# Fetching expert tokens by index: slots by rank, rows from a DRAM copy of x, and a selection by comparison

## The chip, the core and the metric

The kernel runs on one core of a Trainium2 chip. The metric is the time of one execution on the device, in microseconds; the time before is the median of three runs. A profile of one execution gives, for each engine, its instructions with start, length and what they waited for. TensorE is PE in the rows (its weight loads PEld), VectorE DVE, ScalarE ACT, GpSimd POOL, and SP is the engine whose queue issues most DMAs.

## The reference

Two layers over 512 tokens of 1024 columns, in float32. Each layer adds to x an attention branch, a mixture of experts and a gated embedding. The change is in the mixture of experts, where each of 16 experts takes the 64 tokens with the largest affinity to it:

```python
def expert_choice_moe(h, w_router, w1, w3, w2):
    cap = EC_CAPACITY * S // N_EXPERTS                  # 64
    aff = jax.nn.softmax(einsum('bsd,de->bse', h, w_router), axis=-1)
    vals, idx = lax.top_k(aff.transpose(0, 2, 1), cap)  # of each expert
    xg = h[bidx, idx]
    out = (silu(xg @ w1[e]) * (xg @ w3[e])) @ w2[e]
    return zeros_like(h).at[bidx, idx].add(out * vals[..., None])
```

Here h is x after an RMS norm; the expert weights are 1024 x 1024 each, three for each expert.

## The kernel before

x stays in SBUF as four blocks of 128 tokens. The whole program is ordered by a scheduler that runs its own simulation of the engines: within each engine the order is fixed at build time, and a step goes where that simulation finds it ready. `tc.issue_after` only holds a step back behind another one.

**Weights.** `w_tile` issues each 1 MB tile of expert weights as one DMA on SP's queue (L540). The tiles live in a ring of 15 slots (the pool `s8`, shared with a few other tiles), with six more in two small pools for some of the early tiles. A DMA waits until the products that read the slot's last tile are done, so the ring is freed by TensorE, and SP's queue is in order. The first tiles are loaded during the output product of the attention (`GATED`).

**Slots and gathers.** A token's slot at an expert is a number from 1 to 64. For expert 0 it is its rank: the affinities of expert 0 are spread over all partitions by matmuls (L572, the tiles `rowp`), VectorE (L579) and ScalarE (a Sign pass, L580) count greater and equal ones, and `pos0` results. `warm` puts idle matmuls on TensorE over such waits. For the other experts the affinities are transposed (L618), and eight rounds of MAX8 (L628) and MATCH_REPLACE8 (L630) on VectorE mark the 64 largest; a scan over the marks in the order of the sequence gives slots, which four small transposes (L641) bring to `pos`. `gather_one` gathers one expert's tokens: a selection matrix from `iota` and `pos` (L591), times x (L602), copied and transposed (L611, L612). Experts 0 to 3 use it (`ONE`). The other twelve come in two gathers of six (`gather`): x is normalised and split into two parts for each of eight blocks of columns (L682 on ScalarE, L683 on VectorE) and eight matmuls for each block select all six experts' tokens (L686). Gather A is made after expert 3, gather B before expert 7 (`GATHER_B`), and the scheduler lays their blocks between the experts' products.

**Experts.** `hidden(e)` forms tokens times w1 and w3 (L703, 64 matmul records an expert), the SwiGLU (L707 to L709) and its transposes (L712, the tile gT). `down(e)` forms the product with w2 for experts 0 to 3 (L723), whose outputs `scatter` adds to x after expert 7. Experts 4 to 15 keep their activations; their w2 comes afterwards in four quarters of 256 columns (L862, L866), each followed by the scatter (L881) and, beside it, by the gated embedding's products. `where(pr)` gives the scatter its selection for a pair of experts: comparisons with `pos` (L656), four transposes (L659), and the affinities by four small products (L664).

**Queues.** SP issues the weights, ScalarE's queue the biases and the constant `before`. GpSimd issues no DMA; in the experts' stage it has no work before the last sums of the layer.

## Time and profile before

| | us |
|---|---|
| median of 3 runs | 1981.12 |
| range of the runs | 1980.59 to 1981.26 |
| span of the profiled execution | 1978.8 |
| TensorE busy in it | 1901.6 |
| VectorE busy | 778.2 |
| ScalarE busy | 600.8 |
| GpSimd busy | 99.7 |

The profiled span stands 2.3 us under the median of the runs. The two layers have the same course, the second some 977 us after the first; most rows are of the first. In it the experts' first products run from 458 to 798 us, and the four quarters of w2 from there to some 970. TensorE's busy time counts matmuls by modelled ends, and a matmul that is pipelined with the one before it overlaps it, so lengths are read off starts or off busy time by stretch.

### The profile page before, as it was taken

What the parts mean: (1) busy time and instruction counts of PE and PEld (TensorE: products, weight loads), DVE (VectorE), ACT (ScalarE), POOL (GpSimd) and SP (SyncE); (2) the same over time, 40 slices, a digit from 0 to 9 for tenths busy, and PEclk for the clock granted to TensorE, in tenths of its full rate; (3) what the DMA queues carried; (4) which work ended last, traced back from release to release, by engine and by line L of the source; (5) the groups of instructions that cost most, each with busy time, mean ns of one, the idle gap of its engine ahead of it and who ended that gap; (6) DMA issues with size and microseconds to landing.
All of it is one profiled execution on the core that took longest, in us unless ns stands there. A gap on an engine that the chain in (4) does not pass through costs nothing.

```text
span 1978.8 us, 26755 instructions
## 1 busy us (share of the span) xinstructions
PE 1901.6 (96%) x10700; PEld 1239.0 (63%) x10700; DVE 778.2 (39%) x1638; ACT 600.8 (30%) x1257; POOL 99.7 (5%) x156
## 2 busy tenths in 40 slices
PE   7999999999999999999899999999999999999995
PEld 7777777894353333666697677789933533336664
DVE  4655343435141410323657554444342413103336
ACT  3655343331131111231346454433201411112222
POOL 0012110000000000000200121100000000000002
PEclk9999999999999999999999999999999999899998
DMA  5220322479989999989332112234899899999891
GB/s 162 65 75 22 102 80 85 160 287 383 404 339 370 420 419 420 388 318 342 108 102 78 54 46 84 74 98 181 345 358 394 320 411 420 420 413 388 310 322 73
DMA packets 246043, 486.69 MB, mean 246 GB/s; under 512 B 9248, under 2 KB 164384, under 8 KB 245920
## 3 DMA queue, kind: packets, MB, share of 16 engines
q1 hardware_dynamic: 243040, 478.71, 64.7%
q10 hardware_dynamic: 2880, 6.29, 1.0%
q8 instruction: 84, 1.38, 0.3%
q14 instruction: 39, 0.32, 0.0%
HBM read 482.87 MB, written 2.10 MB: 245 GB/s over the span
## 4 chain that ended last, share of the span: by engine, by line
PE 91%; DVE 6%; ACT 1%; issue 1%; DMA 0%; SPq 0%; DVEq 0%; ACTq 0%
PE t L703 22%; PE po L866 9%; PE tokp L152 6%; PE xo L152 5%; PE op L152 5%; PE pg L152 4%; PE po L723 3%; PE sca L881 3%; PE gat L686 2%; PE o L386 2%; PE tp L379 2%; PE gat L602 1%; PE pw L152 1%; PE s L366 1%; PE o L442 1%; PE s L152 1%
## 5 line engine op out<-in xcount | busy, mean ns | idle before, releaser
L703 PE MATMUL t<-w,xg 128*64 128x512 f32 x2048 | 457.5, 598 | 1.6 <-DVE xg L612 1.6
L703 PEld LDWEIGHTS t<-w,xg 128*64 128x64 f32 x2048 | 142.9, 137 | 279.0 <-issue 271.5
L167 DVE TENSOR_TENSOR wl<-raw,wh 128x1024 fp32r<-128x1024 f32 (+2 forms) x116 | 134.6, 1161 | 185.6 <-ACT wh L97 185.0
L866 PE MATMUL po<-s,s 128*64 128x256 f32 x1536 | 188.7, 383 | 0.0
L97 ACT ACTIVATE wh<-raw 128x1024 fp32r<-128x1024 f32 (+2 forms) x116 | 116.7, 1006 | 111.1 <-PE tokp L152 19.7
L866 PEld LDWEIGHTS po<-s,s 128*64 128x64 f32 x1536 | 108.9, 137 | 59.7 <-issue 6.5
L152 PE MATMUL tokp<-wh,s 128*128 128x256 f32 (+1 forms) x640 | 120.4, 287 | 0.0
L708 DVE SCALAR_TENSOR_TENSOR u<-u,t 128x512 f32<-128x512 f32 x32 | 21.9, 686 | 218.0 <-ACT u L707 218.0
L152 PEld LDWEIGHTS tokp<-wh,s 128*128 128x128 f32 x640 | 102.5, 196 | 2.2 <-issue 1.5
L152 PE MATMUL pg<-s,hp 128*128 128x512 f32 x384 | 101.1, 406 | 1.1 <-ACT hp L97 1.1
L152 PE MATMUL xo<-wh,s 128*128 128x256 f32 x512 | 94.9, 285 | 0.0
L152 PE MATMUL tokp<-wl,s 128*128 128x256 f32 (+1 forms) x320 | 91.4, 287 | 0.5 <-DVE wl L167 0.5
L922 POOL TENSOR_TENSOR x<-x,s 128x512 f32<-128x512 f32 x16 | 23.8, 1511 | 1343.1 <-DVE s L920 1338.7
L152 PEld LDWEIGHTS pg<-s,hp 128*128 128x128 f32 x384 | 68.6, 188 | 24.8 <-issue 7.7
L709 DVE TENSOR_TENSOR u<-u,t 128x512 f32<-128x512 f32 x32 | 21.9, 684 | 155.6 <-PE t L703 155.6
L152 PE MATMUL op<-s,wh 128*128 128x512 f32 x256 | 82.2, 397 | 0.0
L152 PEld LDWEIGHTS xo<-wh,s 128*128 128x128 f32 x512 | 80.3, 192 | 0.1
L707 ACT ACTIVATE u<-t 128x512 f32<-128x512 f32 x32 | 19.1, 598 | 195.0 <-PE t L703 195.0
L872 ACT ACTIVATE oh<-po,val 128x256 fp32r<-128x256 f32 x48 | 22.8, 475 | 174.6 <-PE po L866 174.2
L152 PE MATMUL xo<-wl,s 128*128 128x256 f32 x256 | 72.1, 285 | 0.0
L873 DVE SCALAR_TENSOR_TENSOR oh<-po,val,oh 128x256 fp32r<-128x256 f32 x48 | 23.2, 483 | 124.2 <-ACT oh L872 124.2
L152 PEld LDWEIGHTS tokp<-wl,s 128*128 128x128 f32 x320 | 62.5, 195 | 2.1 <-DVE wl L167 1.1
(470 smaller groups left out, 3173.7 us busy)
## 6 DMA issues: line engine op xcount, KB each, us to landing
w<-in_moe_w_dram SPq DMA_DIRECT2D x288, 1024.0 KB, 11.0
s<-in_moe_w_dram SPq DMA_DIRECT2D x96, 1024.0 KB, 10.6
raw<-in_w_in_dram SPq DMA_DIRECT2D x64, 512.0 KB, 3.7
raw<-in_w_out_dram SPq DMA_DIRECT2D x16, 512.0 KB, 3.3
s<-in_ple_gate_w_dram SPq DMA_DIRECT2D x8, 1024.0 KB, 10.4
bias<-in_bias_dram ACTq DMA_DIRECT2D x16, 320.0 KB, 3.1
raw<-in_w_mla_o_dram SPq DMA_DIRECT2D x8, 512.0 KB, 3.3
raw<-in_w_na_o_dram SPq DMA_DIRECT2D x8, 512.0 KB, 3.3
```

The source lines that it names most:

```text
L97: sc.activation(o, i, AF.Copy, scale=scale)
L152: pe.matmul(ps, s_, m_, start=(i == 0), stop=(i == n - 1))
L167: ve.tensor_sub(wl, raw, wh.bitcast(F32))
L379: pe.transpose(tp[:, j, :], pr_[:, j * P:(j + 1) * P], ident)
L386: pe.matmul(o[hh_ * 64:(hh_ + 1) * 64, :], vm[:, j, h * 64:(h + 1) * 64], pts[hh_][:, j, :], start=(j == 0), stop=(j == 3))
L686: pe.matmul(ps, (xh if i % 2 == 0 else xl)[:, i // 2, :], s[:, i // 2].rearrange("p a b -> p (a b)"), start=(i == 0), stop=(i == 7))
L703: products.append(pe.matmul(ps[hf * 64:(hf + 1) * 64, :], xg(k), w[:, k % 2, hf * S:(hf + 1) * S], start=(k == 0), stop=(k == 7)))
L723: pe.matmul(po[hf * 64:(hf + 1) * 64, :], gT[:, k % 4, k // 4, :], w[:, k % 2, hf * S:(hf + 1) * S], start=(k == 0), stop=(k == 7))
L866: pe.matmul(po[ee * CAP:(ee + 1) * CAP, :], gTs[2 * n + ee][:, k % 4, k // 4, :], ws[ee][:, k, :], start=(k == 0), stop=(k == 7))
L873: ve.scalar_tensor_tensor(o[:, 1, :], po, val, o[:, 0, :].bitcast(F32), ALU.mult, ALU.subtract)
L881: pe.matmul(ps[:, j, :], sT[:, (c + j) * P:(c + j + 1) * P], o, start=(i == 0), stop=(i == len(parts) - 1))
L922: (gp if 2 * c + hf in (LAST_POOL if last else ON_POOL) else ve).tensor_tensor(xv, xv, t, ALU.add)
```

## The change

Slots of the first pair (`RANKED = 2`) go by rank: `ranks(e)` is the old code of expert 0 as a function, called for expert 1 too, after the first gather. Only these two experts are gathered by `gather_one`. `before` and `iota` keep their use there.

For all experts the eight rounds now keep the values and, by `max_index`, the places of the 64 largest; the loop's last replacement, the scan and the four small transposes go. Places are turned from the order of the sequence to the order of the kernel's tokens by shifts, and two small products per half bring values and places to `vals`, `places` and `index`, one column for each pair of experts, 128 slots on the partitions.

x is copied to DRAM (`xd`, rows of 1024 columns and one more that holds the token's norm factor `rx`), by eight DMAs on ScalarE's queue. `fetch(pr)` is an indirect DMA on GpSimd's queue that reads the 128 rows of a pair of experts. `turn(pr)` multiplies each row by its factor, transposes it in eight blocks and multiplies by the gains. The fetches of pairs 1 and 2 are issued before the first expert, and each following one when a pair has been turned; a turn is held back behind the products of the last expert of the pair before. The two big gathers go.

`where` compares a new constant, the tokens' numbers, with `places`, which gives the selection in the orientation that the scatter needs; its transposes, its ScalarE copy and the value products go. The rest of the diff takes out comments, renames `GATHER_B` to `SCATTER_AT`, and sets GpSimd's DMA scratch to 2048 bytes.

```diff
+RANKED = 2
...
+    dp = ctx.enter_context(tc.tile_pool(name="dram", bufs=2, space=bass.MemoryType.DRAM))
...
+            gains, lgains, iota, wr, number = (load(n) for n in ("gains", "lgains", "iota", "w_router", "number"))
...
+        xd = dp.tile([S, D + 1], F32, tag="xd", name="xd")
+        for c in range(4):
+            sc.dma_start(xd[c * P:(c + 1) * P, 0:D], x[:, c, :])
+        for c in range(4):
+            sc.dma_start(xd[c * P:(c + 1) * P, D:D + 1], rx[:, c:c + 1])
...
+        def ranks(e):
...
         xg = gather_one(0)
+        for e in range(1, RANKED):
+            ranks(e)
...
-        for _ in range(CAP // 8):
-            m8 = kp.tile([NE, 8], F32, tag="m8", bufs=2, name="m8")
-            ve.max(m8, cur)
-            nxt = row()
-            ve.match_replace(nxt, m8, cur, -1.0)
-            cur = nxt
-        sel = row()
-        ve.tensor_scalar(sel, cur, 0.0, None, ALU.is_lt)
-        cs = row()
-        ve.tensor_tensor_scan(cs, sel, sel, 0.0, ALU.add, ALU.max)
-        ps1 = row()
-        ve.tensor_tensor(ps1.rearrange("e (c r) -> e r c", r=GH), cs.rearrange("e (r c) -> e r c", r=GH),
-                         sel.rearrange("e (r c) -> e r c", r=GH), ALU.mult)
-        pT = psT.tile([P, 4, NE], F32, tag="T", name="pT")
-        for c in range(4):
-            pe.transpose(pT[:, c, :], ps1[:, c * P:(c + 1) * P], ident[:NE, :NE])
-        ve.tensor_copy(pos, pT)
-        ve.tensor_copy(pos[:, :, 0], pos0)
-        if dbg and l == 0:
-            dma(dbg["pos"], pos.rearrange("p c e -> p (c e)"))
-            dma(dbg["aff"], aff.rearrange("p c e -> p (c e)"))
+        best = kp.tile([NE, 2, CAP], F32, name="best")
+        place = kp.tile([NE, CAP], U32, name="place")
+        for i in range(CAP // 8):
+            s_ = slice(8 * i, 8 * i + 8)
+            ve.max(best[:, 0, s_], cur)
+            ve.max_index(place[:, s_], best[:, 0, s_], cur)
+            if i < CAP // 8 - 1:
+                nxt = row()
+                ve.match_replace(nxt, best[:, 0, s_], cur, -1.0)
+                cur = nxt
+        part = kp.tile([NE, CAP], U32, name="part")
+        ve.tensor_scalar(part, place, GW - 1, GH.bit_length() - 1, ALU.bitwise_and, ALU.logical_shift_left)
+        ve.scalar_tensor_tensor(place, place, GW.bit_length() - 1, part, ALU.logical_shift_right, ALU.bitwise_or)
+        ve.tensor_copy(best[:, 1, :], place)
+        pv = psT.tile([P, 2, NE // 2], F32, tag="T", name="pv")
+        for i in range(2):
+            for j in range(2):
+                pe.matmul(pv[j * CAP:(j + 1) * CAP, i, :], best[:, i, :], ident[:NE, j:NE:2], start=(i == 0), stop=(i == 1), skip_group_check=True)
+        vals = ep.tile([P, NE // 2], F32, bufs=1, name="vals")
+        places = ep.tile([P, NE // 2], F32, bufs=1, name="places")
+        index = ep.tile([P, NE // 2], U32, bufs=1, name="index")
+        ve.tensor_copy(index, pv[:, 1, :])
+        ve.tensor_copy(places, pv[:, 1, :])
+        ve.tensor_scalar(vals, pv[:, 0, :], 0.5, None, ALU.mult)
...
         def where(pr):
-            sv = qp.tile([P, 4, 2, CAP], F32, tag="oh", bufs=OHB, name="sv")
-            for c in range(4):
-                ve.tensor_tensor(sv[:, c], bc(pos[:, c, 2 * pr:2 * pr + 2], CAP), iota.unsqueeze(1).to_broadcast([P, 2, CAP]), ALU.is_equal)
-            ps = psT.tile([P, S], F32, tag="T", name="tp")
-            for c in range(4):
-                pe.transpose(ps[:, c * P:(c + 1) * P], sv[:, c].rearrange("p a b -> p (a b)"), ident)
             svT = qp.tile([P, S], F32R, tag="svT", bufs=(NE - BLOCKED) // 2, name="svT")
-            acopy(svT, ps)
-            ps = psT.tile([P, 2], F32, tag="T", name="val")
-            for c in range(4):
-                pe.matmul(ps, sv[:, c].rearrange("p a b -> p (a b)"), aff[:, c, 2 * pr:2 * pr + 2], start=(c == 0), stop=(c == 3))
-            val = qp.tile([P, 1], F32, tag="val", bufs=(NE - BLOCKED) // 2, name="val")
-            for ee in range(2):
-                r = slice(ee * CAP, (ee + 1) * CAP)
-                ve.tensor_scalar(val[r, :], ps[r, ee:ee + 1], 0.5, None, ALU.mult)
-            return svT, val
-        def gather(pool, e0, n):
-            xg = pool.tile([P, 8, n * CAP], F32, tag="xg", bufs=1, name="xg")
-            s = ga.tile([P, 4, n, CAP], F32R, tag="sel", bufs=1, name="sel")
-            for c in range(4):
-                ve.tensor_tensor(s[:, c], bc(pos[:, c, e0:e0 + n], CAP), iota.unsqueeze(1).to_broadcast([P, n, CAP]), ALU.is_equal)
-            for k in range(8):
-                xh = ga.tile([P, 4, P], F32R, tag="xh", name="xh")
-                xl = ga.tile([P, 4, P], F32R, tag="xl", name="xl")
-                for c in range(4):
-                    xv = x[:, c, k * P:(k + 1) * P]
-                    sc.activation(xh[:, c, :], xv, AF.Identity, scale=rx[:, c:c + 1])
-                    ve.scalar_tensor_tensor(xl[:, c, :], xv, rx[:, c:c + 1], xh[:, c, :].bitcast(F32), ALU.mult, ALU.subtract)
-                ps = psS.tile([P, n * CAP], F32, tag="S", name="gat")
-                for i in range(8):
-                    pe.matmul(ps, (xh if i % 2 == 0 else xl)[:, i // 2, :], s[:, i // 2].rearrange("p a b -> p (a b)"),
-                              start=(i == 0), stop=(i == 7))
-                if k % 2:
-                    sc.activation(xg[:, k, :], ps, AF.Identity, scale=g_moe[:, k:k + 1])
-                else:
-                    ve.tensor_scalar(xg[:, k, :], ps, g_moe[:, k:k + 1], None, ALU.mult)
+            ve.tensor_scalar(svT, number, places[:, pr:pr + 1], None, ALU.is_equal)
+            return svT, vals[:, pr:pr + 1]
...
+        def fetch(pr):
+            rows_ = gp_.tile([P, D + 1], F32, tag="rows", bufs=2, name="rows")
+            gp.indirect_dma_start(out=rows_, out_offset=None, in_=xd, in_offset=bass.IndirectOffsetOnAxis(ap=index[:, pr:pr + 1], axis=0))
+            return rows_
+        def turn(rows_):
+            xg = gp_.tile([P, 8, 2 * CAP], F32, tag="xg", bufs=2, name="xg")
+            ve.tensor_scalar(rows_[:, 0:D], rows_[:, 0:D], rows_[:, D:D + 1], None, ALU.mult)
+            for q in range(2):
+                ps = psT.tile([P, 4, P], F32, tag="T", name="tp")
+                for j in range(4):
+                    k = 4 * q + j
+                    pe.transpose(ps[:, j, :], rows_[:, k * P:(k + 1) * P], ident)
+                ve.tensor_tensor(xg[:, 4 * q:4 * q + 4, :], ps, bc(g_moe[:, 4 * q:4 * q + 4], P), ALU.mult)
...
+        fetched = {pr: fetch(pr) for pr in (RANKED // 2, RANKED // 2 + 1)}
+        turned = {}
+        def tokens(e):
+            if e < RANKED:
+                return xg[e]
+            return lambda k: turned[e // 2][:, k, e % 2 * CAP:(e % 2 + 1) * CAP]
+        def next_tokens(e):
+            pr = e // 2 + 1
+            if e % 2 and pr in fetched:
+                with tc.issue_after(products[-1].ins):
+                    turned[pr] = turn(fetched.pop(pr))
+                if pr + 2 < NE // 2:
+                    fetched[pr + 2] = fetch(pr + 2)
...
-            if e < ONE - 1:
+            if e + 1 < RANKED:
                 with tc.issue_after(products[-1].ins):
-                    xg = gather_one(e + 1)
-            else:
+                    xg.append(gather_one(e + 1))
+            next_tokens(e)
+            if e == ONE - 1:
...
-        xgA = gather(ga, ONE, NA_)
...
-            gT = hidden(e, lambda k: xg[:, k, i * CAP:(i + 1) * CAP], kept if e >= BLOCKED else None)
+            gT = hidden(e, tokens(e), kept if e >= BLOCKED else None)
+            next_tokens(e)
...
-    nc = bacc.Bacc("TRN2", target_bir_lowering=False, num_devices=1)
+    nc = bacc.Bacc("TRN2", target_bir_lowering=False, num_devices=1, dynamic_dma_scratch_size=2048)
```

## Rows read from the trace of the kernel before

**Rows 1.** The page: the span; TensorE's busy time, its share and its matmuls; the share of the DMA engines in tenths, over 40 equal slices of the span.

```profile
span 1978.8 us, 26755 instructions
...
PE 1901.6 (96%) x10700; PEld 1239.0 (63%) x10700; DVE 778.2 (39%) x1638; ACT 600.8 (30%) x1257; POOL 99.7 (5%) x156
...
DMA  5220322479989999989332112234899899999891
```

**Rows 2.** Busy time by stretch. Columns: the stretch in us and its length; busy us and instructions of TensorE (PE), its weight loads (PEld), VectorE (DVE), ScalarE (ACT) and GpSimd (POOL); the granted TensorE clock; the busy share of the DMA engines; GB/s. The first six rows are of layer one, the last three of layer two.

```profile
443.00:463.00 20.00, 19.25 (x143) 13.60 (x144) 12.75 (x43) 4.43 (x12) 0.00 (x0) 1.00 0.84 332
463.00:546.00 83.00, 79.30 (x376) 27.79 (x374) 27.47 (x64) 8.84 (x20) 0.00 (x0) 1.00 0.99 401
546.00:612.00 66.00, 66.00 (x324) 35.89 (x322) 26.58 (x74) 24.57 (x70) 0.00 (x0) 1.00 0.87 333
612.00:796.00 184.00, 174.23 (x784) 65.42 (x780) 33.77 (x63) 23.43 (x37) 0.00 (x0) 0.98 1.03 419
796.00:842.00 46.00, 44.88 (x348) 30.57 (x348) 14.40 (x39) 10.76 (x23) 0.00 (x0) 1.00 1.08 387
842.00:884.00 42.00, 42.00 (x298) 28.99 (x296) 10.85 (x18) 12.82 (x28) 0.00 (x0) 1.00 0.86 305
...
1440.00:1523.00 83.00, 79.29 (x370) 27.59 (x368) 26.18 (x61) 8.84 (x20) 0.00 (x0) 0.98 1.00 401
1523.00:1590.00 67.00, 67.00 (x330) 36.27 (x328) 28.19 (x80) 24.58 (x70) 0.00 (x0) 1.00 0.87 326
1590.00:1774.00 184.00, 174.53 (x782) 65.99 (x780) 33.77 (x63) 23.44 (x37) 0.00 (x0) 0.97 1.03 419
```

**Rows 3.** The waits of SP's DMA queue from 460 to 620 us: which line waited for whom, us in total, times, the longest. L540 issues the expert weights, t is written by the first products (L703), po by the second (L723).

```profile
SPq L540 <- PE t L703: 110.0, 46, 15.9
SPq L540 <- PE po L723: 32.9, 11, 7.6
```

**Rows 4.** The waits of TensorE's weight loads from 740 to 800 us, the row on DMA, with the same columns.

```profile
PEld t L703 <- DMA w<-in_moe_w_dram: 1.0, 2, 0.8
```

**Rows 5.** TensorE's instructions in order of time, in layer one, merged where alike: start, length (us), engine, line, operation, tiles, shape, count, and in brackets the idle time before and what ended it. First the start of the experts' stage, then its end and the end of the first quarter of w2.

```profile
458.31 13.95 PE L703 MATMUL t<-w,xg 128*64 128x512 f32 x64
474.99 0.39 PE L641 MATMUL pT<-ident,row 16*128 16x16 f32 x4 [2.73 <-DVE row L637]
475.31 0.66 PE L712 MATMUL gT<-ident,u 128*128 128x128 f32 x4
...
488.05 13.95 PE L703 MATMUL t<-w,xg 128*64 128x512 f32 x64 [0.78 <-DVE xg L612]
...
506.75 7.09 PE L723 MATMUL po<-w,gT 128*64 128x512 f32 x32
...
768.50 13.95 PE L703 MATMUL t<-w,xg 128*64 128x512 f32 x64
...
783.89 14.06 PE L703 MATMUL t<-w,xg 128*64 128x512 f32 x64
...
833.64 3.67 PE L866 MATMUL po<-s,s 128*64 128x256 f32 x30
...
838.25 1.70 PE L881 MATMUL sca<-oh,svT 128*128 128x256 f32 x12
```

**Rows 6.** Busy time of TensorE by single lines, each asked for alone over a stretch (columns: stretch, length, PE busy, PEld busy, clock, DMA share, GB/s). In this order: the matmuls of the big gathers (L686); of the one-expert gathers after the first (L602); their transposes (L611); the selection's transposes (L659) in the scatter of the first pairs and in the first quarter; the selection's value products (L664) in the same two places; the rows of the first rank (L572).

```profile
458.00:800.00 342.00, 24.41 (x128) 21.91 (x128) 0.99 0.98 393
...
458.00:800.00 342.00, 11.87 (x48) 3.58 (x48) 0.99 0.98 393
...
458.00:800.00 342.00, 2.41 (x12) 1.23 (x12) 0.99 0.98 393
...
640.00:675.00 35.00, 1.73 (x8) 1.28 (x8) 1.00 1.03 421
...
798.00:842.00 44.00, 3.86 (x24) 2.65 (x24) 1.00 1.08 387
...
640.00:675.00 35.00, 2.18 (x16) 2.13 (x16) 1.00 1.03 421
...
798.00:842.00 44.00, 5.89 (x48) 5.82 (x48) 1.00 1.08 387
...
443.00:463.00 20.00, 2.02 (x16) 1.86 (x16) 1.00 0.84 332
```

**Rows 7.** Groups of VectorE instructions by line, tile and shape: count, busy us, mean ns of one, and the idle time before them.

```profile
L167 DVE TENSOR_TENSOR wl<-raw,wh 128x1024 fp32r<-128x1024 f32 x96 | 117.6, 1225 | 166.5 <-ACT wh L97 166.1
...
L628 DVE MAX8 m<-row 16x8 f32<-16x512 f32 x16 | 10.9, 681 | 0.6
...
L630 DVE MATCH_REPLACE8 row<-m,row 16x512 f32<-16x512 f32 x16 | 10.6, 662 | 0.0
```

**Rows 8.** ScalarE's instructions in order of time: two DMA issues on its queue, and the first Sign pass of the first rank, with the idle time before it.

```profile
321.59 0.98 ACTq L547 DMA_DIRECT2D before<-in_before_dram  x2
...
449.00 0.66 ACT L580 ACTIVATE junk<-rowp,na 128x512 f32<-128x512 f32 x1 [2.93 <-PE rowp L572]
```

**Rows 9.** The DMAs issued on L540 over the whole span: us from issue to landing, least, median and most.

```profile
DMA to landing us min/median/max: 4.7/11.0/18.8
```

**Rows 10.** Busy time by stretch around the embedding's product in layer one, columns as in rows 2.

```profile
718.00:722.00 4.00, 1.12 (x5) 0.60 (x5) 2.75 (x4) 2.49 (x3) 0.00 (x0) 1.00 1.02 420
...
724.00:730.00 6.00, 5.75 (x14) 2.59 (x14) 0.00 (x0) 0.80 (x2) 0.00 (x0) 0.50 1.03 422
```

More of the change, by code (lines that the diff above doesn't have):

```diff
@@ L562, in trunk @@
         ve.tensor_tensor(aff, lgs, bc(sm, NE), ALU.mult)
-        warm(WARM[1], m_lg)
-        rowp = []
-        for _ in range(2):
-            rowp.append(psT.tile([P, S], F32, tag="T", name="rowp"))
-            for c in range(4):
-                m = pe.matmul(rowp[-1][:, c * P:(c + 1) * P], aff[:, c, 0:1].to_broadcast([P, P]), ident, start=(c == 0), stop=(c == 3), skip_group_check=True)
-        warm(WARM[0], m)
-        na = small.tile([P, 4], F32, tag="nm4", name="na")
-        ve.tensor_scalar(na, aff[:, :, 0], -2.0 ** 60, None, ALU.mult)
@@ L576, in trunk @@
-        junk, junk2 = (psS.tile([P, S], F32, tag="S", name="junk") for _ in range(2))
-        rank = small.tile([P, 2, 4], F32, tag="ss16", name="rank")
-        for c in range(4):
-            ve.scalar_tensor_tensor(junk, rowp[0], aff[:, c, 0:1], before[c // 2][:, c % 2, :], ALU.is_equal, ALU.mult, accum_out=rank[:, 0, c:c + 1])
-            sc.activation(junk2, rowp[1], AF.Sign, scale=2.0 ** 60, bias=na[:, c:c + 1], accum_out=rank[:, 1, c:c + 1])
-        pos0 = ep.tile([P, 4], F32, bufs=1, name="pos0")
@@ L761, in trunk @@
         gTs, pw = [], []
+        gt = ExitStack()
+        gp_ = gt.enter_context(tc.tile_pool(name=f"ga{l}", bufs=2, side="right", reuse_waits="tile"))
+        fetched = {pr: fetch(pr) for pr in (RANKED // 2, RANKED // 2 + 1)}
[11 more added lines that the diff above has]
+                    fetched[pr + 2] = fetch(pr + 2)
+        xg = [xg]
         for e in range(ONE):
[L764 removed]
+            gT = hidden(e, tokens(e))
             if e % 4 == 0 and e < BLOCKED:
                 outputs()
[L767 removed]
+            if e + 1 < RANKED:
                 with tc.issue_after(products[-1].ins):
[L769 to L770 removed]
+                    xg.append(gather_one(e + 1))
+            next_tokens(e)
+            if e == ONE - 1:
                 ft.close()
@@ L969, in _constants @@
         "iota": np.tile(np.arange(1, CAP + 1, dtype=f), (P, 1)),
+        "number": np.tile(np.arange(S, dtype=f), (P, 1)),
     }
```

50 lines of the change are left out of this document (27 added, 23 removed).

## The prediction

> **What bounds the kernel now.** I read the page first: TensorE (PE) is busy for 96% of the span, and the DMA line stands near full in the ten slices of each layer that hold the mixture of experts [rows 1]. Two resources near their limit mean that the average decides nothing, so I cut the expert stage into stretches. The reader is to see in each row whether PE or the DMA engines have room. From 463 to 546 us the engines move 401 GB/s, from 546 to 612 only 333, from 612 to 796 again 419 with a share of 1.03 [rows 2]. I take 420 GB/s as what they can do with these 4 KB rows. The dip lies where the big gather A stands on PE. Why the queue stops there is in its own waits: between 460 and 620 us SP waits 110.0 us for the expert products and 32.9 us for the second products to free a buffer [rows 3]: the ring is full because PE spends its time on gathers. At the other end the reverse holds. The last expert's products take 14.06 us where others take 13.95, and the weight loads wait 1.0 us for DMA there [rows 4, 5]: the last weights come just in time. So in the hidden stage (first products to the last expert's, 458.31 to 797.95, 339.6 us) both end together, and work taken from PE is worth only what DMA can follow. After that come four quarters of w2. The first runs at 387 GB/s with a DMA share of 1.08, the limit for its 1 KB rows. The second has PE busy 42.00 of 42 us and a share of 0.86: PE sets its end [rows 2]. What is won up to the end of the first quarter is kept.
>
> **The change, part by part, for one layer.**
>
> *PE.* Gone in the hidden stage: gathers A and B, 128 matmuls, 24.4 us; two of three one-expert gathers of that stretch, 2/3 of 11.87 = 7.9, with their transposes, 2/3 of 2.41 = 1.6; the selection's transposes and value products inside the scatter of the first pairs, 1.73 + 2.18 = 3.9 [rows 6]; the 2.73 us wait for the selection after the first expert and the 0.78 us wait before the second [rows 5], as expert 1 now has its slots by rank, ready before the first products end. Sum 41.3. The product that turns values and places replaces the four small transposes behind that wait, at their 0.39 us. Added: seven pairs with two groups of four transposes, each 0.66 like the four of gT [rows 5], 9.2; the second rank's rows, 2.0 as for the first [rows 6]. Net 30.1. In the first quarter six more selections go: 3.86 + 5.89 = 9.75 [rows 6]. New on the path of each pair is the scaling of the fetched rows on VectorE: the nearest row is a 128x1024 operation, 1.23 us [rows 7]. If none of it is covered, seven cost 8.6. PE's stage is then 309.5 to 318 us.
>
> *DMA, weights.* The same weights move. Without the dips the stretch 463 to 796 needs 333 us less 83 x 19/420 = 3.8, less 66 x 87/420 = 13.7, less 0.4: 17.9 less, 315.1 us. In layer two the same rows give 3.8 + 15.0 + 0.4 = 19.2. Lower bound for this gain: nothing, if the ring blocks as before; I take the whole, because a tile waits for products some fourteen tiles of the ring back, those of experts 2 and 3 where the dip begins, and PE reaches these some 10 us sooner (3.5 us of waits and two gathers of 4.8, less what is added).
>
> *DMA, new traffic.* Seven fetches of 128 rows of 4,100 bytes are 3.67 MB, all inside the stretch that is now at its limit: 8.7 us at 420 GB/s, 9.5 at the 387 of the 1 KB rows. Nothing in this trace is fetched through an index, so the upper end is open; twice the low end is my bound, 17.5. I take 9.5, the price of the slower of two streams seen. The copy of x, 2.1 MB, is 5.0 us, but from 443 to 463 the engines have 20 x 88/420 = 4.2 us to spare, as the ring is full until the first products begin [rows 2]: 0.8 net, between 0 and 5. The column of factors is 2 KB; I set it in that 0.8.
>
> *The start of the products.* The eight copies go out from ScalarE's queue, where two issues took 0.98 us together [rows 8], so 2.7 to 3.9 us. Queued behind them are the Sign passes of the first rank, on which all of PE waits. ScalarE idles 2.93 us just before these [rows 8] and I put the issues there and ahead; 0 to 3. The second rank's rows and its buffers come between the first gather and the first products: 0 to 2.0 us of PE. Together I take 1.0 us; it delays the release of the ring as well, so it counts in full.
>
> *GpSimd's queue.* The fetches wait there for the index and the copy of x; behind them GpSimd has nothing until the last sums of the layer, 400 us on. Their use waits on PE: rows of pair 1 are needed when expert 1's products end, by the rows near 458.3 + 1 + 13.95 + 5.4 + 7.1 + 13.95 = 499.7 [rows 5, 6]. The index is late: eight new index searches at the 0.68 us of the maximum [rows 7] lengthen VectorE's chain by 5.4 us, and the second rank holds both transpose banks some 4 us longer. The bank is free at about 463; eight maxima and searches at 0.68 and seven replacements at 0.74 with their gaps make 17 us, the other work of VectorE in that stretch 3.5, the product and its copies 1.5: about 485. A fetch lands 4.7 to 18.8 us after its issue if it fares like the weights [rows 9], 490 to 504, and is scaled in 1.2: this turn stalls PE 0 to 6 us. The later ones are fetched two experts, 30 us, ahead. PE is ahead of DMA by more than that (below), so I cost it at nothing; without that cover it is 6.
>
> *The first quarter.* Thirteen DMAs of 1.05 MB at 387 GB/s take 35.2 us after the last hidden tile, at 796.0. Then one pair's products, 3.67, and the scatter's end, 2.7: 41.5 us. Now it ends at 838.25 + 1.70 = 839.95 [rows 5], 43.95 after that tile. Gain 2.5; 0 if PE is late, 9.75 if DMA had room.
>
> *Elsewhere.* The new constant of 0.26 MB is 0.6 us in the queue ahead of the first weights of the program, once. The splits on ScalarE and VectorE that fed the big gathers go; neither engine was the bound, so nothing.
>
> **Sum.** Layer one 17.9 + 2.5 - 9.5 - 0.8 - 1.0 = 9.1; layer two 19.2 + 2.5 - 11.3 = 10.4; once -0.6: 18.9 us. The profiled span 1978.8 becomes 1959.9. It stands 2.3 us under the median of the runs, 1981.1, which I keep: **1962.2 us**. After it DMA is the bound to the end of the first quarter, and PE has 30.1 + 9.75 - 8.6 - 1 - 9.1 = 21 us of slack per layer. This forecast's own range is 1957 (low fetch, free start) to 1978 (double fetch).
>
> **Rivals.**
> - *PE stays the bound.* Then all of its work comes back: 2 x (30.1 + 9.75 - 1) - 0.6 = 77, 1904 us. The 419 GB/s over 184 us speaks against it. 4 in 100.
> - *The pauses stay.* If buffers are still freed late, and half of the dip is filled, 9 + 2.5 - 11.3 leaves about nothing: 1981. For it: fifteen slots are shared with other tiles. 10 in 100.
> - *Slower, the fetch.* Place: the DMA engines in the hidden stage. A layer has 17.9 + 2.5 - 1.8 = 18.6 us to spend on seven fetches, so it decides at 2.7 us each, against 1.36 taken. If a row of 4,100 bytes that starts at no round address costs four times its share, 5.4 us, a layer loses 7 x 5.4 - 18.6 = 19 us: 2020. Against it: rows of 1 KB cost only 8% more than those of 4 KB [rows 2]. 8 in 100.
> - *Tokens late.* If each turn holds PE by 4.5 us, in its order, seven are 31.5, the 21 us of slack are gone and 10 more with them: 1981. VectorE is busy for a third to a fifth of the stage [rows 2], so it is no queue to wait in, which speaks against it. The Trainium skill's page "SBUF — State Buffer" (Who interferes with whom) has a rule against this change: descriptors of DMAs from GpSimd's queue are written by GpSimd, and some VectorE operations between SBUF and SBUF lock it out while they run. No row here shows it. As each such operation here lasts 1.3 us at most, my price stays under the 4.5. 6 in 100.
> - *The lower clock.* PE now waits for weights: eight tiles of 2.5 us an expert against the 15.39 us from one expert's products to the next [rows 5]. Waits have cost the clock before: in 718 to 722 PE worked 1.12 of 4 us, and the granted clock then fell to 0.50, the 1.2 GHz level, until 730 [rows 10], while the 2.73 us wait in layer one left it at 1.00 [rows 2, 5]. A slow stretch costs half its length, so it needs over 42 us of them a layer to eat the 21. With 80 us, half of the last eight experts at 20 us each, 40 are lost, 19 more than the slack, against a gain of 9.5: 2 x 9.5 slower, 2000. The Trainium skill's page "TensorE: Matmul & The Clock Gate" (HAM oscillation) describes such a loop, bursts parted by waits for DMA, each run at the lower clock. By it the chance would be more; but a slow PE is a full one, and catches up. 4 in 100.
>
> **How the numbers follow.** Forecast 68 in 100, the rivals 4, 10, 8, 6 and 4. The range is 1952 to 1984: it holds the forecast, with some of the first quarter's 9.75 at its low end, and the two cases near 1981, and leaves out 16 in 100. A difference of 0.2%, 4 us, is what a measurement can tell from none. Faster by more: 0.68 + 0.04 and 0.02 of the pauses' 0.10, 0.74; slower: 0.08 + 0.04 and 0.01 of the late tokens' 0.06, 0.13; within: the rest, 0.13.
>
> **What would show it.** Right: 463 to about 789 with no stretch under 410 GB/s; the products of later experts 20 us apart instead of 15.3, with waits for weights where none were; TensorE's busy share falling below 92% while the span falls by 1%. The fetch: seven issues a layer on GpSimd's queue, 3.7 MB. Wrong: DMA still dipping below 350 GB/s after 546 (pauses stay); weight loads waiting for xg rather than for DMA (tokens late); DMA share at its limit but fewer GB/s from 612 on (fetch dear); granted clock well below 0.97 over the stage.

## The result and the profile after

The changed kernel takes 1993.09 us (median of 4 runs) against 1980.86 for the kernel before in the same sessions, a ratio of 1.0061 (95% interval 1.0047 to 1.0074): 12 us slower, where 19 us faster were forecast. The profiled execution took 1992.9 us, its span 1991.0.

The page of the changed kernel: the span, TensorE's share, the DMA engines in 40 slices, and the queues of ScalarE (q10) and GpSimd (q0) with packets, MB and share of the engines.

```profile
span 1991.0 us, 25665 instructions
...
PE 1853.8 (93%) x10324; PEld 1182.4 (59%) x10324; DVE 745.9 (37%) x1468; ACT 549.4 (28%) x1109; POOL 113.3 (6%) x170
...
DMA  5220322488999999999332113235979999999891
...
q10 hardware_dynamic: 5184, 10.49, 1.7%
q0 software_dynamic: 2016, 7.35, 1.0%
```

TensorE has 47.8 us less to do than in [rows 1], and the kernel is slower all the same. The stretches say where, with the columns of [rows 2]; the first five are of layer one, the next of layer two.

```profile
443.00:463.00 20.00, 16.31 (x122) 13.02 (x123) 7.96 (x31) 4.14 (x11) 0.00 (x0) 0.91 1.01 359
463.00:546.00 83.00, 72.39 (x338) 25.84 (x337) 31.56 (x74) 8.27 (x17) 3.01 (x3) 0.94 0.89 345
546.00:612.00 66.00, 64.80 (x292) 23.91 (x288) 23.77 (x40) 7.46 (x12) 1.17 (x1) 1.00 1.03 420
612.00:796.00 184.00, 163.09 (x726) 58.09 (x728) 24.60 (x34) 18.56 (x30) 2.80 (x3) 0.98 1.03 420
796.00:842.00 46.00, 37.52 (x263) 20.69 (x260) 8.76 (x13) 5.64 (x9) 0.00 (x0) 1.00 1.07 387
...
1440.00:1523.00 83.00, 72.99 (x349) 27.32 (x346) 31.95 (x76) 8.44 (x18) 2.90 (x3) 0.93 0.88 342
```

From 546 us on the DMA engines do what was forecast: 333 GB/s became 420, and TensorE has 1.2 and 21 us to spare in two stretches that were full or nearly so. The sign that later experts would begin 20 us apart holds for some of them alone. From expert 6 to expert 15 they begin 15.3 to 29.3 us apart, 19.6 on average, where the kernel before has 15.3 to 26.8 and 18.8. TensorE stops for weights from 658 to 719 us and at the last expert; there it stops eight products at a time, as in these rows in order of time:

```profile
667.57 1.94 PE L706 MATMUL t<-w,xg 128*64 128x512 f32 x8 [0.55 <-DMA w<-in_moe_w_dram]
670.21 1.94 PE L706 MATMUL t<-w,xg 128*64 128x512 f32 x8 [0.70 <-DMA w<-in_moe_w_dram]
```

The seven fetches a layer are there (7.35 MB in both); only TensorE's share is 93%, not under 92 as forecast, and it is 94% in the run latecol below, which has no slow stretch here. The loss is ahead of that stretch: 463 to 546 fell from 401 to 345 GB/s, and TensorE is idle there for 10.6 us. Its instructions in order of time show two holes:

```profile
455.36 1.27 PE L616 MATMUL gat<-x,s 128*64 128x256 f32 x6 [3.48 <-DVE s L605]
...
478.52 3.60 PE L616 MATMUL gat<-x,s 128*64 128x512 f32 x16
489.73 0.38 PE L662 MATMUL pv<-ident,best 16*64 16x8 f32 x4 [7.61 <-DVE best L647]
490.04 1.11 PE L715 MATMUL gT<-ident,u 128*128 128x128 f32 x4
491.10 0.38 PE L662 MATMUL pv<-ident,best 16*64 16x8 f32 x4
491.85 1.11 PE L625 MATMUL tp<-ident,xt 128*128 128x128 f32 x4 [0.36 <-ACT gT L100]
492.89 8.93 PE L726 MATMUL po<-w,gT 128*64 128x512 f32 x32
501.65 1.88 PE L706 MATMUL t<-w,xg 128*64 128x512 f32 x8
```

The second is the larger. pv, the product that turns values and places, stands in TensorE's order ahead of gT, which needs only hidden(0), and of down(0), which needs gT. It waits 7.61 us for VectorE's last maximum, and all of these wait with it, though u, which gT reads, is ready at 480.2. Then the transposes take 1.11 us in place of the 0.66 of [rows 5] and down(0) 8.93 in place of 7.09: the granted clock is at 0.50, the 1.2 GHz level, after the hole (the columns as above).

```profile
486.40:496.64 10.24, 6.55 (x26) 3.28 (x28) 5.66 (x17) 0.60 (x1) 2.08 (x2) 0.50 0.38 122
```

DMA moves 122 GB/s in that time, since the ring is full: SP's queue waits for the expert products of both kinds to free a buffer (460 to 505 us, columns as in [rows 3]).

```profile
SPq L543 <- PE po L726: 21.3, 4, 17.4
SPq L543 <- PE t L706: 19.9, 9, 7.8
```

What made pv late is on VectorE. It copies aT, the transposed affinities with which the rounds start, at 471.17, where the kernel before did so at 458.41, because aT comes behind the second rank; and each of eight rounds has grown by a search. First the row of the kernel before, then those of the changed one:

```profile
458.41 0.68 DVE L625 COPY row<-aT 16x512 f32<-16x512 f32 x1 [0.27 <-PE aT L618]
...
471.17 0.67 DVE L642 COPY row<-aT 16x512 f32<-16x512 f32 x1
...
472.66 0.67 DVE L647 MAX8 best<-row 16x8 f32<-16x512 f32 x1
...
473.45 0.67 DVE L648 FIND_INDEX8 place<-best,row 16x8 uint32<-16x512 f32 x1
...
474.11 0.67 DVE L651 MATCH_REPLACE8 row<-best,row 16x512 f32<-16x512 f32 x1
```

The first hole, 3.48 us ahead of 455.36, comes from ScalarE's queue. The issues of the last two column writes span 5.99 us, and the Sign passes of the first rank stand behind them (the bracket names VectorE's passes beside them, which end at 450.8; in the run col below the Sign pass begins while they still run, so it does not wait for them):

```profile
445.17 5.99 ACTq L571 DMA_DIRECT2D xd<-rs_y  x2
451.27 0.66 ACT L593 ACTIVATE junk<-rowp,na 128x512 f32<-128x512 f32 x1 [5.86 <-DVE junk L592]
```

**The account.** To find all of the 12 us I cut each kernel's trace at the first router product (lg), the first products of expert 0 (h0) and of expert 1 (h1), the end of the last expert's, and the first transpose after each quarter. In us, layer one / layer two:

| | lg to h0 | h0 to h1 | h1 to the end of the hidden stage | first quarter | second quarter |
|---|---|---|---|---|---|
| before | 50.68 / 50.68 | 29.75 / 31.45 | 309.90 / 310.61 | 45.10 / 45.08 | 42.21 / 42.21 |
| after | 55.86 / 55.27 | 38.84 / 38.96 | 303.30 / 303.59 | 43.41 / 43.02 | 42.22 / 45.69 |

So 4.9 and 8.3 us a layer are lost ahead of h1 (means of the two layers), 6.8 won behind it and 1.9 in the first quarter. One more change stands at the end: layer two's second quarter takes 45.69 us. TensorE's order of the same products differs there (scatter products right behind the products whose split ScalarE still makes); 1.3 us of it are waits, and where the rest goes stays open. Values from 42.2 to 45.7 turn up in either layer in the runs below whatever their edit, so I judge them by the stages, and times by more than these 3.5 us.

### The profile page after: what moved, and what is told of

Read it like the earlier page. It is cut to its first block, busy times and chain, and to the rows that moved or that the text cites. A ratio compares the mean times of both kernels' runs of the same rounds, so it can differ in the third digit from the quotient of the medians.

```text
span 1991.0 us, 25665 instructions
## 1 busy us (share of the span) xinstructions
PE 1853.8 (93%) x10324; PEld 1182.4 (59%) x10324; DVE 745.9 (37%) x1468; ACT 549.4 (28%) x1109; POOL 113.3 (6%) x170
## 3 DMA queue, kind: packets, MB, share of 16 engines
q0 software_dynamic: 2016, 7.35, 1.0%
## 4 chain that ended last, share of the span: by engine, by line
PE 78%; DMA 13%; DVE 6%; ACT 2%; issue 1%; SPq 0%; ACTq 0%; DVEq 0%
PE t L706 15%; DMA w<-in_moe_w_dram 9%; PE po L883 8%; PE tokp L155 6%; PE xo L155 5%; PE op L155 5%; PE pg L155 4%; PE po L726 3%; DMA s<-in_moe_w_dram 3%; PE sca L898 2%; PE o L389 2%; PE tp L382 2%; PE pw L155 1%; PE s L369 1%; PE o L445 1%; PE s L155 1%
## 5 line engine op out<-in xcount | busy, mean ns | idle before, releaser
L706 PE MATMUL t<-w,xg 128*64 128x512 f32 x2048 | 462.7, 598 | 23.9 <-DMA w<-in_moe_w_dram 23.9
L706 PEld LDWEIGHTS t<-w,xg 128*64 128x64 f32 x2048 | 138.7, 137 | 315.3 <-issue 245.3
L100 ACT ACTIVATE wh<-raw 128x1024 fp32r<-128x1024 f32 (+2 forms) x116 | 116.7, 1006 | 112.2 <-PE tokp L155 19.2
L889 ACT ACTIVATE oh<-po,vals 128x256 fp32r<-128x256 f32 x48 | 22.8, 474 | 199.3 <-PE po L883 199.3
L890 DVE SCALAR_TENSOR_TENSOR oh<-po,vals,oh 128x256 fp32r<-128x256 f32 x48 | 23.2, 483 | 145.2 <-ACT oh L889 145.2
L898 PE MATMUL sca<-oh,svT 128*128 128x256 f32 x384 | 61.3, 295 | 6.4 <-ACT oh L889 4.0
L100 ACT ACTIVATE s<-gT 128x512 f32<-128x512 f32 x24 | 14.3, 597 | 188.3 <-PE gT L715 188.3
```

Of the source, the lines that this page charges most:

```text
L100: sc.activation(o, i, AF.Copy, scale=scale)
L706: products.append(pe.matmul(ps[hf * 64:(hf + 1) * 64, :], xg(k), w[:, k % 2, hf * S:(hf + 1) * S], start=(k == 0), stop=(k == 7)))
L889: sc.activation(o[:, 0, :], po, AF.Identity, scale=val)
L890: ve.scalar_tensor_tensor(o[:, 1, :], po, val, o[:, 0, :].bitcast(F32), ALU.mult, ALU.subtract)
L898: pe.matmul(ps[:, j, :], sT[:, (c + j) * P:(c + j + 1) * P], o, start=(i == 0), stop=(i == len(parts) - 1))
```

## The experiments

The table has what was measured; the texts on record and what follows stand behind it. Ratios are to the kernel before in the same session (its medians lie between 1980.9 and 1982.3 us), with 95% intervals; the stages are those of the profiled execution.

| run | us | ratio | lg to h0 | h0 to h1 | h1 to end | second quarter |
|---|---|---|---|---|---|---|
| late | 1977.42 | 0.9980 [0.9969, 0.9990] | 56.24 / 55.29 | 29.30 / 29.30 | 303.44 / 303.61 | 45.71 / 45.69 |
| col | 1986.74 | 1.0027 [1.0017, 1.0036] | 51.24 / 51.23 | 38.39 / 39.47 | 302.66 / 302.02 | 45.70 / 45.69 |
| first | 1984.26 | 1.0016 [1.0007, 1.0026] | 54.79 / 55.22 | 36.59 / 36.13 | 303.91 / 303.89 | 42.22 / 42.22 |
| all3 | 1966.17 | 0.9921 [0.9904, 0.9937] | 50.68 / 50.68 | 29.14 / 29.14 | 305.19 / 305.45 | 43.25 / 42.23 |
| latecol | 1964.82 | 0.9921 [0.9904, 0.9938] | 51.24 / 51.23 | 29.30 / 29.30 | 303.50 / 303.01 | 45.69 / 42.22 |
| warm | 1992.03 | 1.0051 [1.0034, 1.0067] | 55.72 / 55.42 | 37.44 / 37.43 | 303.50 / 304.34 | 45.71 / 42.23 |
| warm28 | 1993.06 | 1.0062 [1.0045, 1.0079] | 55.76 / 55.41 | 36.34 / 36.34 | 304.90 / 304.47 | 45.69 / 44.25 |
| noidx | 1979.36 | 0.9992 [0.9982, 1.0001] | 55.30 / 55.82 | 33.25 / 33.14 | 302.22 / 302.37 | 42.22 / 43.23 |
| nofetch | 1975.13 | 0.9972 [0.9962, 0.9981] | 55.53 / 55.49 | 39.20 / 39.30 | 295.82 / 295.49 | 42.22 / 42.22 |
| all3nofetch | 1950.47 | 0.9848 [0.9832, 0.9864] | 50.68 / 50.67 | 29.14 / 29.14 | 296.55 / 296.78 | 42.23 / 45.70 |
| all3nocopy | 1965.65 | 0.9923 [0.9906, 0.9939] | 50.68 / 50.68 | 29.14 / 29.14 | 304.83 / 305.00 | 43.23 / 42.22 |
| blk2 | 1983.91 | 1.0008 [0.9998, 1.0017] | 51.41 / 51.26 | 38.45 / 38.98 | 304.16 / 303.65 | 42.22 / 45.69 |

### late: pv behind the second products of expert 0

```diff
+            if e == 0:
+                with tc.issue_after(m_po.ins):      # the last matmul of down(0)
+                    find()                          # pv, index, places, vals
...
+                fetched.update((pr, fetch(pr)) for pr in (RANKED // 2, RANKED // 2 + 1))
```

> The pv products (and the copies, the fetches' issue behind them) are held back behind the last matmul of down(0); all traffic is as in the changed kernel (1993.1). Theory (TensorE's order: pv stands ahead of gT and down(0) and waits 7.6 us for VectorE's selection, the clock halves for 10.2 us behind it, and the ring, being full, leaves the DMA engines idle): the wait goes, down(0) takes 7 us again instead of 8.9, hidden(1) starts some 10 us earlier than 501.65 (at 490 to 493), and 7 to 10 us a layer come off: 1973 to 1979. Rival (the traffic of the copy and the fetches is the loss, and a late start is made up for because the DMA engines are the bound behind it): within 2 us of 1993.

15.7 us came off; h0 to h1 fell by 9.5 and 9.7 us, to 29.30, under the kernel before. By the stages it is 9.0 and 9.6 us a layer, of which a second quarter of 45.7 in layer one takes 3.5 back. VectorE's chain is as long as it was; only nothing in TensorE's order waits for it. The rival falls.

```profile
482.55 0.66 PE L715 MATMUL gT<-ident,u 128*128 128x128 f32 x4
...
483.89 6.22 PE L726 MATMUL po<-w,gT 128*64 128x512 f32 x26 [0.35 <-ACT gT L100]
...
492.27 0.40 PE L668 MATMUL pv<-ident,best 16*64 16x8 f32 x8
```

### col and blk2: fewer transfers on ScalarE's queue

```diff
-        for c in range(4):
-            sc.dma_start(xd[c * P:(c + 1) * P, D:D + 1], rx[:, c:c + 1])
+        sc.dma_start(xd[:, D:D + 1].rearrange("(c p) o -> p (c o)", p=P), rx)
```

> The norm column of xd is written by one DMA in place of four, the bytes are the same. Theory (the fourth column write stands in ScalarE's queue until the fourth block of x has landed, at 450.84, and the Sign passes of the first rank stand behind it): the Sign passes start at about 448.4, hidden(0) 3 to 4 us earlier, and as pv then waits for VectorE all the same (its chain starts with the second rank, which also moves up), 3 to 4 us a layer come off: 1985 to 1988. Rivals: the traffic alone costs, no change (1993); or the landing of xd holds the passes by itself, no change either, with the Sign passes still at about 451.

As the theory has it: 6.4 us off, and h0 4.6 and 4.0 us earlier after lg. By the stages it is 5.7 and 5.1 us a layer; a first quarter of 45.6 us and a second of 45.7 take part of it back. ScalarE in order of time in this run: the one issue, then the Sign pass 2.93 us behind the rank's rows, as in [rows 8].

```profile
445.57 0.40 ACTq L570 DMA_DIRECT2D xd<-rs_y  x1
...
449.69 0.66 ACT L592 ACTIVATE junk<-rowp,na 128x512 f32<-128x512 f32 x1 [2.93 <-PE rowp L583]
```

The third and fourth block of x land at 451.7 and 454.65 there, after the Sign pass has begun, so their landing does not hold it by itself. Why then did the fourth write wait? It was issued 0.02 us after the third block had landed, not the fourth as the text above has it (450.84 after 450.82; 1433.65 after 1433.63 in layer two).

```diff
-        for c in range(4):
-            sc.dma_start(xd[c * P:(c + 1) * P, 0:D], x[:, c, :])
+        for c in range(0, 4, 2):
+            sc.dma_start(xd[c * P:(c + 2) * P, 0:D].rearrange("(c p) d -> p c d", p=P), x[:, c:c + 2, :])
```

> The changed kernel with the four blocks of x copied by two DMAs of two blocks each; the four column writes stay. In the changed kernel the fourth column write is issued 0.02 us after the third block has landed, in both layers, with five transfers of ScalarE's queue on the way. Theory A (the wait comes from the number of transfers on the way on that queue, five being all it takes): four at most are on the way here, no wait, the Sign passes start 2.9 us after the rows' products as in the run with one column DMA, and 3 us a layer come off: 1985 to 1989. Theory B (the last column write waits for the second half of x itself to land): it waits as before or longer, to 451 or later, and the time stays within 3 us of 1993.

With two transfers fewer on the way, the same four writes go out without a wait, and the stage begins as early as in col; 9.2 us came off, a little more than theory A has, and theory B falls.

```profile
446.65 0.99 ACTq L571 DMA_DIRECT2D xd<-rs_y  x2
449.81 0.66 ACT L593 ACTIVATE junk<-rowp,na 128x512 f32<-128x512 f32 x1 [2.93 <-PE rowp L584]
```

That does not yet show that the number on the way is the reason, and the semaphores in the traces give another. A semaphore is a counter on which an engine's queue can wait. Each transfer of SP's and ScalarE's queues raises one of eight when it lands, and the next transfer with the same one is issued only after that landing (in all 563 pairs of the changed kernel's trace that can be read). The fourth column write has the third block's semaphore (number 100 in layer one, 107 in layer two), waits for it, and goes out with its landing; in blk2 no column write has the semaphore of a transfer still on the way. SP's weights, which read nothing of xd, wait for blocks of x in the same way (waits of SP's queue from 440 to 460 us, columns as in [rows 3]):

```profile
SPq L543 <- DMA xd<-x: 9.3, 3, 6.5
```

So the program's allotment of semaphores made the wait; theory A's count of five came out right without being the reason. No run changes the allotment alone.

### first: the selection ahead of the second rank

```diff
-        for e in range(1, RANKED):
-            ranks(e)
         aT = psT.tile([P, S], F32, tag="T", name="aT")
...
         ve.tensor_copy(cur.rearrange(...), aT[:NE, :].rearrange(...))
+        for e in range(1, RANKED):
+            ranks(e)
```

> aT and the start of the selection are put ahead of the second rank, so that VectorE's chain need not wait for the second rank's two banks; the work is the same. Theory (pv is late since the chain starts at 471.2 in place of 458.4): the chain starts near 463, its end comes 6 to 8 us earlier, pv waits 0 to 2 us in place of 7.6, the clock's fall behind it goes, and 6 to 9 us a layer come off: 1975 to 1981. Rival (the chain is late for its own length, max_index above all): the wait shrinks by less than 3 us and the time stays over 1987.

A miss, between the theory and its rival: the chain does start 9.2 us earlier, at 462.01, but pv still waits 3.99 us and the clock still falls. By the stages 2.7 and 2.6 us a layer come off; the rest of the 8.8 us is the second quarter.

```profile
486.60 0.38 PE L662 MATMUL pv<-ident,best 16*64 16x8 f32 x4 [3.99 <-DVE best L647]
486.91 1.11 PE L715 MATMUL gT<-ident,u 128*128 128x128 f32 x4
```

The second rank's passes now lie inside the chain, and the first of them itself waits 2.49 us on VectorE for its rows, with the chain behind it. Of the 9.2 us won at the start, pv gets 3.1; the rest was given back in the same queue. VectorE's rows:

```profile
462.01 0.68 DVE L640 COPY row<-aT 16x512 f32<-16x512 f32 x1 [0.27 <-PE aT L632]
...
466.75 0.76 DVE L592 SCALAR_TENSOR_TENSOR junk<-rowp,aff,before 128x512 f32<-128x512 f32 x1 [2.49 <-PE rowp L584]
```

### noidx: a shorter chain

```diff
+        gp.memset(place, 0)
...
-            ve.max_index(place[:, s_], best[:, 0, s_], cur)
+            if i == 0:
+                ve.max_index(place[:, s_], best[:, 0, s_], cur)
```

> The changed kernel with max_index in the first of the eight rounds alone; the places of the seven other rounds are zeros, so those tokens are fetched from row 0 and scattered there (part of the computation is changed), the traffic is the same. It shortens VectorE's chain by seven times 0.75 us, 5.2 us, and leaves its start at 471. Theory (pv stands in TensorE's order and waits for the chain, whatever makes it late): the wait falls from 7.6 to 2 to 3 us, the clock keeps up, hidden(1) starts 8 to 10 us earlier, 6 to 9 us a layer come off: 1975 to 1981. Rival (the place of pv is a symptom, and traffic the loss): over 1988.

The time is as expected, 13.7 us less; the way there is only in part. The wait is 3.83 us in place of 7.61, longer than the 2 to 3 expected, down(0) still takes 8.60 us, and h0 to h1 is 5.6 and 5.8 us shorter, not 8 to 10. By the stages it is 7.2 and 6.5 us a layer; holding pv back gives 9.0 and 9.6 with all the searches in place. So it is the place of pv against the end of the chain that counts, from either side.

```profile
486.14 0.40 PE L664 MATMUL pv<-ident,best 16*64 16x8 f32 x8 [3.83 <-DVE best L648]
```

### warm and warm28: the clock alone

```diff
+                if e:
+                    warm(40, m_gat)      # warm28: 28
```

> The changed kernel with forty products of 128 columns, whose result nobody reads, between the second gather and pv: TensorE is kept busy over some 4.6 us of its 7.6 us wait, the wait itself stays. If the halved clock is part of the loss: no stretch at 0.50 at 486 to 497, down(0) takes about 7.1 us in place of 8.9, the transposes 0.66 in place of 1.11, hidden(1) starts 3 to 5 us earlier, and 3 to 5 us a layer come off 1993: 1983 to 1987. Rival (the wait alone costs, and the full ring gives the slow stretch back later): within 2 us of 1993.

> As the run with forty idle products between the second gather and pv, with twenty-eight, since the forty lasted 9.2 us, longer than the 7.6 us wait that they were to fill: twenty-eight last 6.4 us and end before the selection does. The clock should stay at 1.00 from 482 on, so this prices the fall alone. Theory, from the parts of that run at full clock (down(0) 7.09 in place of 8.93, gT 0.66 in place of 1.11, the four transposes 0.63 in place of 1.11): hidden(1) starts 2.5 to 3 us earlier after hidden(0) than in the changed kernel (36 in place of 38.8), and 2 to 3 us a layer come off 1993: 1987 to 1989. If it stays within 2 us of 1993, the fall of the clock costs nothing by itself.

The first was mis-sized: forty idle products took 9.2 us and outlasted the wait (each leaves two records of 0.115 us, and I had counted one). The second fits. TensorE's rows: 6.52 us of them, and a wait of 1.16 left.

```profile
483.36 6.52 PE L142 MATMUL warm<-x,ident 128*128 128x128 f32 x56
491.03 0.28 PE L664 MATMUL pv<-ident,best 16*64 16x8 f32 x4 [1.16 <-DVE best L649]
```

The same stretch as above, columns as in [rows 2]:

```profile
486.40:496.64 10.24, 8.40 (x60) 5.54 (x60) 6.37 (x17) 0.60 (x1) 0.00 (x0) 1.00 0.35 123
```

The clock stays at 1.00, and h0 to h1 is 2.5 and 2.6 us shorter, as expected of the clock, but h1 to the end is 1.6 and 0.9 longer, as DMA still moves 123 GB/s in that stretch. The stages shrink by 1.0 and 1.6 us (1.3 and 0.6 with forty), and neither time moves by more than 1.1 us, as the rival has it. So the fall of the clock was no more than 1 to 2 us a layer of the loss; most of what late gives back was the hole.

### all3 and latecol: the edits together

> The three edits together: one column DMA, the selection ahead of the second rank, pv behind down(0). Theory (the start of each layer's experts is the whole loss, and from there on the forecasted gain holds): hidden(0) starts at about 459, hidden(1) at 486 to 488, 12 to 14 us a layer come off: 1965 to 1969, some 13 us under the kernel before. Rival (traffic): over 1988. If the DMA engines bound the stage from its start, part of the 13 us a layer is lost to waits for weights, and the time lies between, at 1972 to 1980.

> Two of the three edits, without the third: pv behind down(0), and one column DMA; the selection stays behind the second rank. If the places of pv and of the Sign passes are the whole loss, this comes to the time of the three edits (1966), within 3 us, though VectorE's chain ends 5 to 8 us later. If the early selection matters by itself even with pv held back (xg of expert 1 stands behind the chain on VectorE), hidden(1) starts 1 to 3 us a layer later: 1969 to 1973.

Two edits give all of it, as the text on latecol has it: latecol is at 1964.8 us, 0.9921 [0.9904, 0.9938] of the kernel before, and the third edit adds nothing (by the stages all3 is 1.0 and 1.7 us a layer behind latecol). The stages shrink by 14.0 and 14.3 us against the changed kernel, where late (9.0, 9.6) and col (5.7, 5.1) alone add up to 14.7 and 14.7. In latecol TensorE goes through with no wait over 0.4 us (its rows in order of time) and the DMA engines are near their limit from the start (stretches, columns as in [rows 2]):

```profile
477.07 0.66 PE L714 MATMUL gT<-ident,u 128*128 128x128 f32 x4
477.62 0.44 PE L624 MATMUL tp<-ident,xt 128*128 128x128 f32 x2
478.41 6.22 PE L725 MATMUL po<-w,gT 128*64 128x512 f32 x26 [0.35 <-ACT gT L100]
484.56 0.44 PE L624 MATMUL tp<-ident,xt 128*128 128x128 f32 x2
484.93 1.93 PE L725 MATMUL po<-w,gT 128*64 128x512 f32 x6
486.79 0.40 PE L667 MATMUL pv<-ident,best 16*64 16x8 f32 x8
487.12 2.37 PE L705 MATMUL t<-w,xg 128*64 128x512 f32 x10
```

```profile
463.00:546.00 83.00, 80.01 (x382) 27.52 (x380) 32.64 (x75) 10.44 (x21) 3.32 (x3) 1.00 1.02 413
546.00:612.00 66.00, 64.17 (x293) 23.86 (x289) 21.91 (x34) 5.62 (x9) 2.11 (x2) 1.00 1.02 420
612.00:796.00 184.00, 158.07 (x708) 55.15 (x710) 23.32 (x32) 19.08 (x30) 1.88 (x2) 0.99 1.03 418
```

pv itself is not free yet: VectorE ends the selection at 486.06, 0.7 us ahead of it.

### nofetch, all3nofetch and all3nocopy: the traffic

```diff
-            gp.indirect_dma_start(out=rows_, ..., in_=xd, ...)                  # nofetch, all3nofetch
-            ve.tensor_scalar(rows_[:, 0:D], rows_[:, 0:D], rows_[:, D:D + 1], None, ALU.mult)
+            ve.tensor_scalar(rows_[:, 0:D], x[:, pr % 4, :], vals[:, 0:1], None, ALU.mult)
...
-        xd = dp.tile([S, D + 1], F32, tag="xd", name="xd")                      # all3nocopy
-        for c in range(4):
-            sc.dma_start(xd[c * P:(c + 1) * P, 0:D], x[:, c, :])
...
-            gp.indirect_dma_start(out=rows_, ..., in_=xd, ...)
+            gp.indirect_dma_start(out=rows_[:, 0:D], ..., in_=a["x"], ...)
```

> The changed kernel without the seven fetches a layer, the turn reading a block of x in their place (part of the computation is changed); pv's wait and the late first rank stay. With the three edits in, the same cost 15.7 us (7.9 a layer). If fetch and late start are separate terms that add: 1993 less 14 to 17, 1976 to 1979, still only some 3 us under the kernel before for a kernel that fetches nothing. Rival (the late start leaves the ring so full that the bytes of the fetches are hidden there): 1985 or more.

> The kernel with the three edits (1966.2), without the seven fetches a layer: the turn reads a block of x in place of the fetched rows (part of the computation is changed), the copy of x to DRAM is still written. If the DMA engines bound the stage and the fetches cost what their bytes cost (9.5 us a layer forecasted; 3.7 MB at 420 GB/s are 8.8): 7 to 9.5 us a layer come off: 1947 to 1952. Rival (the fetches ride in gaps, TensorE bounds): within 4 us of 1966. If they cost by rows (128 short ones of 4 KB for each fetch), more: under 1945.

> The kernel with the three edits (1966.2), without the copy: the rows are fetched from the kernel's input x, unscaled (part of the computation is changed), so the traffic of the fetches stays and the 2.1 MB of the copy and its norm column go, and ScalarE's queue has four issues and one fewer ahead of the first rank. If the copy was rightly costed at 0.8 us a layer: 1962 to 1966. Rival (the DMA engines are full from 443 on, so that the copy's bytes cost their own time, 2.1 MB at 400 GB/s are 5 us, and its 512 words of the column more): 4 to 7 us a layer come off, 1952 to 1958. A second rival: tokens wait for the landing of the copy nowhere, so that by itself changes nothing.

The fetches cost 7.5 us a layer by the stages in the changed kernel (18.0 us by the runs, a little over the 14 to 17 expected, 3.5 of them the second quarter) and 8.7 with the three edits (15.7 by the runs). Their bytes at 420 GB/s are 8.7 us, so being rows found by an index adds nothing that shows. They add to the late start, they don't hide in it. The copy costs 0.4 us a layer by the stages, with the one column write of the three edits.

## Why the forecast was wrong

The step that failed is in the prediction's *PE* paragraph: "the 2.73 us wait for the selection" was counted as gone, and the product that turns values and places only "replaces the four small transposes behind that wait, at their 0.39 us". The product replaced them in the same place of TensorE's order, and it waits for the same chain, which I had myself found longer and later: "about 485" for the index, in the paragraph on GpSimd. I charged that lateness to the fetch alone ("this turn stalls PE 0 to 6 us ... I cost it at nothing"), and asked who waits behind the fetch, but not who waits behind pv. By the prediction's own rows hidden(0) and the second gather end near 458.3 + 1 + 13.95 + 4.0, at 477, so a pv that is ready at 485 is an 8 us hole. Measured: 7.61, with the chain at 489.6 and TensorE there at 482.1. h0 to h1, 26.5 us in the GpSimd paragraph's sum (13.95 + 5.4 + 7.1), took 38.8: the hole and the clock's fall behind it, 2.5 by warm28, are 10.1 of the 12.3 more.

A second step failed ahead of it, in *The start of the products*: 1.0 us forecast, 5.2 and 4.6 measured. The range of "0 to 3" for ScalarE's queue priced the issues, not a wait for a landing inside them; col gives 4.6 and 4.0 of it back.

The other terms, a layer:
- *The pauses*, 17.9 and 19.2 less: the dip is gone. 333 became 420 GB/s, and in latecol 463 to 796 moves 413 to 420. "The pauses stay" is refuted. No run prices the term alone.
- *The fetches*, 9.5: 7.5 and 8.7 measured; the rival of a dear fetch, 5.4 us each, is refuted. *The copy*, 0.8: 0.4.
- *The hidden stage as a whole*, 6.6 and 7.9 less (the sum without the first quarter and the constant): it grew by 7.7 and 5.1; in latecol it shrank by 6.3 and 9.2. The forecast's balance of bytes was right to 1.3 us a layer.
- *The first quarter*, 2.5 less: 1.7 and 2.1; in latecol 2.3 and 2.3. "What is won up to the end of the first quarter is kept" held but for the second quarter's order, which no step foresaw: 3.5 us of layer two.
- *Tokens late*: no turn held TensorE for rows; its waits ahead of L693 (the turn's transposes) from 500 to 800 us are 1.6 us in all, for ScalarE's copies of gT. The fourteen issues of fetches took 0.93 to 1.17 us. By the Trainium skill's page "SBUF — State Buffer" (Who interferes with whom) some VectorE operations could lock GpSimd out while it writes a fetch's descriptors; no run here shows it.
- *The lower clock*: from 546 to 796 us it is at 0.50 once, for 6.8 us from 725.3, where the embedding's products begin and the kernel before has the same. The waits for weights from 658 to 719 us (L706 waits 11.6 us in layer one, 1.4 at the longest) left it at 1.00. The loop that the Trainium skill's page "TensorE: Matmul & The Clock Gate" (HAM oscillation) describes did not come. The other falls of the stage followed the two holes.

The forecast time, 1962.2, is 2.6 us from latecol, which does all that the change does, with pv in another place and the column in one write. Without the 3.5 us that its second quarter of layer one loses, the balance would be out by 1 us. Some of that is luck: layer one falls 0.5 us short of its forecast and layer two goes 1.1 beyond. So the mechanism was right from the second expert on, and two waits ahead of it were overlooked: pv's, and the one inside ScalarE's issues.

## What to carry to other kernels

A product fed by another engine's chain is a wait for all that stands behind it in TensorE's order: work out when the chain ends and when TensorE gets there, both by rows, and put the product behind work that needs nothing from it. When a chain is lengthened, charge its lateness to every reader of its result, the in-order ones first. An issue of a copy on a computing engine's queue can wait for an earlier landing, with that engine's work behind it: look up which semaphore it waits for and which transfer raises that, and write a column with one DMA.

## What was not expected of the hardware

- The last transfer of the copy on ScalarE's queue was issued only when the third had landed, which has the same semaphore: 5.4 and 4.9 us behind the exponentials that it followed, in the two layers. It is so in each of the seven runs that copy x in eight transfers.
- The column writes, 0.5 KB of 4-byte words each, took a median of 11.5 us to land, the 512 KB blocks 7.8.
